# Two PSUM tiles for the transposed squares of layer 1's token tiles, shared out by reading engine instead of by half

## The chip, the cores and the metric

The kernel runs on one core of a Trainium2 chip. The metric is device time in microseconds (us): the median of three runs, 1484.73 us for the kernel before. One execution was also taken by the hardware profiler; the durations in this document come from it.

## The reference

The reference is a model of two layers over 512 latent tokens and 256 context tokens of width 1024 (768 tokens, six tiles of 128). Layer 0 mixes by a long convolution and by attention, layer 1 by a chunked mLSTM. Each layer normalizes the tokens, scales and shifts them by numbers computed from the condition, projects, mixes, and adds the result back:

```python
for layer in range(DEPTH):
    sh_l, sc_l, ga_l = adaln(c, w_mod[layer], b_mod[layer])
    sh_c, sc_c, ga_c = adaln(c_ctx, w_mod[layer], b_mod[layer])
    h_lat = rms_norm(x_lat, g_pre[layer]) * (1 + sc_l[:, None]) + sh_l[:, None]
    h_ctx = rms_norm(x_ctx, g_pre[layer]) * (1 + sc_c) + sh_c
    ...
    x_lat = x_lat + ga_l[:, None] * rms_norm(y_lat, g_post[layer])
```

The change touches the place where layer 1's `h_lat` and `h_ctx` are made and turned round, so that the model dimension lies on the partitions for the projection `h @ w_in`.

## The kernel before, in words

Everything is computed in 32 bits on TensorE by splitting each operand into a high and a low part and taking three products (`mm3`). The program is written in regions. In a region the calls on an engine are first recorded and then issued in an order written out by hand in a table (`record` and `play`, L988 to L1001; tables `ORDERS`, the one for this place is `ORDERS["out0"]`, L436 to L474). `play` also asks for that order to be kept on each engine, so the five engines' own orders are fixed numbers. Every recorded instruction is issued by one helper, which is why all rows of the profile carry its line, L998. The names of tiles tell the rows apart.

Region "out0" is the last part of layer 0: the output projection and, token tile by token tile (4, 5, 0, 1, 2, 3), the function `epi0` (L2203 to L2220). It adds the gated, normalized result to the tokens (`xt`), squares and sums them on ScalarE (`junk`, `ss`), and has VectorE write the normalized tokens in two halves of 512 columns (`xn`). Then comes `h_tile` (L1165 to L1180). For each half, TensorE transposes four squares of 128 x 128 into PSUM (`pm`, written by a matmul with the identity `c_ident`). ScalarE scales and shifts squares 0 and 1 of the half into `hf`, VectorE squares 2 and 3. `hf` holds all eight squares of a token tile and has one buffer. At last `split` (L1003 to L1005) makes the high part `hTh` on ScalarE (a CAST) and the low part `hTl` on VectorE, half by half; both are operands of layer 1's projections.

Between the transposes the order table puts TensorE's other work: the matmuls of layer 0's output projection (`pj` from `yoh`, `yol`), and, once tiles 4, 5, 0 and 1 are split, layer 1's first value projections (`pj` from `hTh`, `hTl`, with 288 columns). VectorE also collects the output projection (`yacc`), splits weights (`wl`), and after the last token tile makes sums (`zs`, `uu`) and the gate inputs (`wa`), which TensorE transposes next.

In the hand order TensorE doesn't transpose a tile's halves one after the other in all cases: in tiles 4, 0 and 3 squares of the two halves come in turns. "The second half" here is the one that comes later in the order.

Waits are set from the tiles: an instruction waits for earlier instructions of other engines on the same PSUM tile, whichever part of it they touch, two reads included. A PSUM tile here is one bank of 512 32-bit numbers on each partition, that is four squares. `pm` has four such places, and a table (`"pm@11"`, L826) says which tile goes to which.

Of the kernel before, what the change touches and what calls it, by code (L numbers as in the profile page):

```python
# [9 lines left out]
AF = mybir.ActivationFunctionType  # L10
ALU = mybir.AluOpType
# [3 lines left out]
P = 128  # L15
# [886 lines left out]
def _body(tc, ins, outs):  # L902
# [9 lines left out]
    def uid(s):  # L912
        cnt[0] += 1
        return f"{s}_{cnt[0]}"
# [13 lines left out]
    def T(pl, tag, shape, dt=F32, bufs=None):  # L928

        b = bufs or bufs_of.get(id(pl)) or 1  # L930
        name = uid(tag)
        if b > 1:
            key = f"{tag}@{pools.setdefault(id(pl), (len(pools), pl))[0]}"
            n = turn_of[key] = turn_of.get(key, -1) + 1
            order = SLOTS.get(key)
            tag, b = f"{tag}_{order[n] if order else n % b}", 1
        kw = {} if bufs is None and b == 1 else {"bufs": b}
        return pl.tile(list(shape), dt, tag=tag, name=name, **kw)

    def PJ(shape=(P, 512)):  # L940
        return T(pp.pj, "pj", shape)

    def PM(shape=(P, 512)):
        return T(pp.pm, "pm", shape) if pp.pm is not pp.pj else PJ(shape)
# [35 lines left out]
    V, S, TE = Engine("vector", pinv), Engine("scalar", pinv), Engine("tensor", pin)  # L980
# [22 lines left out]
    def split(hi, lo, src):  # L1003
        S.copy(hi, src)
        return V.tensor_tensor(lo, src, f(hi), ALU.subtract).ins  # L1005
# [50 lines left out]
    def const(name, shape, dt=F32, src=None, eng=None):  # L1056
        t = cp.tile(list(shape), dt, tag="c_" + name, name="c_" + name)
        (eng or G).dma_start(t, src if src is not None else ins[name])
        return t
# [3 lines left out]
    ident = const("ident", (P, P), eng=S)  # L1063
# [85 lines left out]
    scl = [cp.tile([P, KT, 2], F32, tag=f"scl{l}", name=f"scl{l}") for l in range(2)]  # L1149
    shf = [cp.tile([P, KT, 2], F32, tag=f"shf{l}", name=f"shf{l}") for l in range(2)]  # L1150
# [12 lines left out]
    turns = [[] for _ in range(6)]  # L1163

    def h_tile(pl, i, xn, scl, shf):  # L1165

        c = 0 if i < 4 else 1
        hf = T(pl, "hf", (P, KT, P))
        for hh in range(2):
            ps = PM((P, 4, P))  # L1170
            for t in range(4):
                turns[i].append(TE.transpose(ps[:, t, :], xn[hh][:, t * P:(t + 1) * P], ident).ins)
            for t in range(4):
                ft = hh * 4 + t
                if t < 2:
                    S.activation(hf[:, ft, :], ps[:, t, :], AF.Identity, bias=shf[:, ft, c:c + 1], scale=scl[:, ft, c:c + 1])
                else:
                    V.tensor_scalar(hf[:, ft, :], ps[:, t, :], scl[:, ft, c:c + 1], shf[:, ft, c:c + 1], ALU.mult, ALU.add)
            sl = slice(hh * 4, hh * 4 + 4)
            split(hTh[:, sl, i * P:(i + 1) * P], hTl[:, sl, i * P:(i + 1) * P], hf[:, sl, :])  # L1180

# [5 lines left out]
    def proj_seg(w, c, s):  # L1187

        ps = PJ()
        _, a, n = SEGS[s]  # L1190
        for kt in range(KT):
            mm3(ps[:, :n], tuple(x[:, kt, c * P:(c + 1) * P] for x in w), hcols(kt, a, a + n), kt == 0, kt == KT - 1)
        return ps

    def proj_feat(w, c, turned=False):
        if turned:
            return [proj_seg(w, c, s) for s in (1, 0)][::-1]
        return proj_seg(w, c, 0), proj_seg(w, c, 1)
# [58 lines left out]
    for d in 'x0 x1 z x3 x2 x4 W00 x5 s0 h0 s1 s2 h1 h2 W01 s3 h3 W10 W11'.split():  # L1257
# [13 lines left out]
        elif d[0] == "h":  # L1271
            u = int(d[1])
            if u < 3:
                t = [T(xp, "xt", (P, 4, 256), bufs=6) for _ in range(2)]
            else:
                t = rawa[:, 8:12], rawb[:, 0:4]
# [370 lines left out]
    for j in range(8):  # L1647
        w = load_w(ew[2 * j]) if j else None
        x1c = T(hp, "tmp", (P, NT))
        ps = proj_feat(w, 0) if j else ps0[:2]  # L1650
# [7 lines left out]
        ps = ps0[2:]  # L1658
        if j:
            ps = []  # L1660
# [10 lines left out]
        ps = proj_feat(w, 0)  # L1671
# [14 lines left out]
        for s, a, n in SEGS:  # L1686
            R = n // P
            ps = proj_seg(w, 1, s)
# [27 lines left out]
    for i in range(6):  # L1716
        ps = PJ()[:, :256]
# [54 lines left out]
    for c in range(2):  # L1772
        t = cg[c]
        V.tensor_tensor(t, rope[:, 0], grow[:, c:c + 1].broadcast_to([P, 4, P]), ALU.mult)
        t = sg[c]
# [265 lines left out]
    for n in range(24):  # L2041
# [3 lines left out]
        for b in range(2):  # L2045
# [6 lines left out]
            if n in (18, 19):  # L2052
                c = 2 * (n - 18) + b
# [149 lines left out]
    def epi0(i, rs):  # L2203
        xt = T(op, "xt", (P, D), bufs=2)
        SP.dma_start(xt, ins["x"][i])
        for hf, y in enumerate((yacc0, yacc1)):
            sl = slice(hf * 512, (hf + 1) * 512)
            V.scalar_tensor_tensor(xt[:, sl], y[:, i], rs, xt[:, sl], ALU.mult, ALU.add)
        if i < 4:
            SP.dma_start(x1d[i], xt)  # L2210
        ss = T(op, "ss", (P, 1), bufs=2)
        xn = [T(op, "xn", (P, 512), bufs=3) for _ in range(2)]
        junk = T(op, "junk4", (P, D), mybir.dt.bfloat16, bufs=1)
        S.activation(junk, xt, AF.Square, accum_out=ss)
        rs = T(op, "rs", (P, 1), bufs=2)
        tmp = T(op, "sst", (P, 1), bufs=2)
        rstd(rs, ss, D, tmp)
        for hf in range(2):
            V.tensor_scalar(xn[hf], xt[:, hf * 512:(hf + 1) * 512], rs, None, ALU.mult)
        return lambda: h_tile(op, i, xn, scl[1], shf[1])  # L2220
# [673 lines left out]
```

## Time and profile before

| | us |
|---|---|
| three runs, median (lowest to highest) | 1484.73 (1484.15 to 1485.28) |
| profiled execution, whole | 1486.4 |
| span of its instructions | 1484.6 |
| TensorE (PE) busy in the span | 1448.9 |
| VectorE (DVE) busy | 1071.1 |
| ScalarE (ACT) busy | 778.8 |

The profile was taken at a mean granted TensorE clock of 0.999 of full speed. Busy time is not the same as time on the path to the end: an engine that is busy half the time can still make another wait. The rows further down show which. In a row of the timeline several like instructions in direct sequence stand together (x4); the start is that of the first, the length that of all of them. Matmul ends are modelled and overlap, so matmuls are followed from start to start.

### The profile page before, as it was taken

The numbers are of one execution on the slowest core, as the hardware profiler recorded it, in microseconds if no ns is written. First come the engines' busy times: TensorE is split into PE (matmuls) and PEld (weight loads), VectorE is DVE, ScalarE is ACT, GpSimd is POOL, SyncE is SP. The second block draws the span as 40 slices with busy tenths as digits, with TensorE's granted clock in tenths as the row PEclk, the third lists the DMA queues.
The fourth block names the chain that finished last, engine by engine and source line by source line (L and its number), as shares of the span: only waits on it lengthen the run. The fifth ranks groups of instructions, "written<-read, shape, count | busy, mean of one in ns | idle before, by whom it ended". The sixth has DMA issues, their size and how long they took to land. (4 is left out here: it accounts for less than half of the span.)

```text
span 1484.6 us, 25597 instructions
## 1 busy us (share of the span) xinstructions
PE 1448.9 (98%) x10122; PEld 1320.5 (89%) x10122; DVE 1071.1 (72%) x1971; ACT 778.8 (52%) x1587; POOL 95.2 (6%) x141
## 2 busy tenths in 40 slices
PE   7999999999999999999999989999999999999997
PEld 5888998989998998989997779999999999989776
DVE  6687777887865666668334899666777777778698
ACT  5643443344435444446332567655766666766554
POOL 1100000001000000000000100000000101110000
PEclk9999999999999999999999999999999999999999
DMA  9655556557331121233463343676654647476575
GB/s 380 212 139 151 142 138 165 147 127 185 86 103 43 55 96 47 90 118 104 152 217 98 114 144 129 228 257 211 221 166 114 161 126 166 141 199 179 203 256 215
DMA packets 63687, 230.93 MB, mean 156 GB/s; under 512 B 7707, under 2 KB 9243, under 8 KB 60784
## 3 DMA queue, kind: packets, MB, share of 16 engines
q1 hardware_dynamic: 55000, 198.63, 38.9%
q0 software_dynamic: 7696, 29.50, 11.3%
q8 instruction: 79, 1.29, 0.3%
q10 hardware_dynamic: 872, 1.18, 0.2%
q14 instruction: 40, 0.33, 0.1%
HBM read 207.23 MB, written 68.19 MB: 186 GB/s over the span
## 5 line engine op out<-in xcount | busy, mean ns | idle before, releaser
L998 PE MATMUL pj<-wl,hTh 128*128 128x256 f32 (+2 forms) x1104 | 315.4, 291 | 1.9 <-DVE wl L998 1.9
L998 PE MATMUL pj<-wh,hTh 128*128 128x256 f32 (+2 forms) x1104 | 316.2, 293 | 0.8 <-ACT qjunk L998 0.4
L998 PE MATMUL pj<-wh,hTl 128*128 128x256 f32 (+2 forms) x1104 | 313.8, 291 | 0.0
L998 PE MATMUL pj<-hTh,wh 128*128 128x512 f32 (+1 forms) x832 | 286.7, 347 | 0.1
L998 PE MATMUL pj<-hTl,wh 128*128 128x512 f32 (+1 forms) x832 | 285.5, 344 | 0.6 <-DVE hTl L998 0.6
L998 PE MATMUL pj<-hTh,wl 128*128 128x512 f32 (+1 forms) x832 | 285.2, 345 | 0.0
L998 DVE TENSOR_TENSOR wl<-wr,wh 128x1024 fp32r<-128x1024 f32 (+1 forms) x154 | 187.6, 1222 | 48.5 <-ACT wh L998 45.7
L998 PEld LDWEIGHTS pj<-wl,hTh 128*128 128x128 f32 x1104 | 206.9, 189 | 7.4 <-DVE wl L998 2.9
L998 PEld LDWEIGHTS pj<-wh,hTh 128*128 128x128 f32 x1104 | 205.9, 188 | 7.4 <-issue 2.0
L998 PEld LDWEIGHTS pj<-wh,hTl 128*128 128x128 f32 x1104 | 206.0, 188 | 4.3 <-issue 1.1
L998 ACT CAST wh<-wr 128x1024 fp32r<-128x1024 f32 (+1 forms) x154 | 159.0, 1044 | 95.5 <-PE pj L998 61.7
L998 PEld LDWEIGHTS pj<-hTh,wh 128*128 128x128 f32 x832 | 156.6, 189 | 19.2 <-DVE vl L998 0.9
L998 PEld LDWEIGHTS pj<-hTh,wl 128*128 128x128 f32 x832 | 156.3, 188 | 18.2 <-DVE wl L998 0.2
L998 PEld LDWEIGHTS pj<-hTl,wh 128*128 128x128 f32 x832 | 156.7, 189 | 17.4 <-DVE hTl L998 0.9
L998 DVE TENSOR_TENSOR PTl<-pj,PTh 128x384 fp32r<-128x384 f32 (+1 forms) x80 | 41.1, 525 | 18.8 <-ACT PTh L998 18.3
L998 ACT CAST PTh<-pj 128x384 fp32r<-128x384 f32 (+1 forms) x80 | 35.5, 458 | 30.6 <-PE pj L998 30.0
L998 DVE TENSOR_TENSOR wl<-ch,wh 128x1024 fp32r<-128x1024 f32 x28 | 34.2, 1221 | 24.1 <-ACT wh L998 24.0
L998 DVE TENSOR_REDUCE mx<-s 128x1 f32<-128x768 f32 (+1 forms) x48 | 37.2, 774 | 11.4 <-PE s L998 11.2
L998 PE MATMUL pm<-Rh,dfa 128*128 128x256 f32 (+1 forms) x192 | 44.9, 305 | 0.0
L998 POOL DMA_DIRECT2D o_sums<-in_o_w_in x28 | 22.8, 814 | 333.9 <-DMA o_sums<-in_o_w_in 167.2
L998 DVE TENSOR_TENSOR med<-big 128x512 f32<-128x512 f32 (+1 forms) x48 | 40.4, 865 | 5.0 <-ACT big L998 4.7
L998 PE MATMUL s<-dfa,qTh 128*128 128x256 f32 (+1 forms) x160 | 42.8, 338 | 0.7 <-ACT hdh L998 0.6
(397 smaller groups left out, 3250.3 us busy)
## 6 DMA issues: line engine op xcount, KB each, us to landing
wr<-in_e_w_in SPq DMA_DIRECT2D x52, 512.0 KB, 5.0
wr<-in_o_w_in SPq DMA_DIRECT2D x50, 512.0 KB, 6.4
o_sums<-in_o_w_in POOLq DMA_DIRECT2D x28, 512.0 KB, 6.7
ch<-o_sums SPq DMA_DIRECT2D x21, 512.0 KB, 4.8
wh<-in_w_mod SPq DMA_DIRECT2D x10, 1024.0 KB, 8.4
wl<-in_w_mod SPq DMA_DIRECT2D x9, 1024.0 KB, 7.6
wr<-in_e_w_out SPq DMA_DIRECT2D x16, 512.0 KB, 4.0
w_sums<-in_o_w_out POOLq DMA_DIRECT2D x16, 512.0 KB, 7.6
```

Source lines behind the costliest of these rows:

```text
L998: x = fn(*a, **k)
```

## The change

Before, each half of a token tile has a PSUM tile of its own, and ScalarE and VectorE both read from it. After, the two PSUM tiles are taken at the head of the function; one receives squares 0 and 1 of both halves, which ScalarE reads, the other squares 2 and 3 of both halves, which VectorE reads. The arithmetic, the number of instructions and each engine's order stay the same.

```diff
--- before.py
+++ after.py
@@ -1166,16 +1166,17 @@
 
         c = 0 if i < 4 else 1
         hf = T(pl, "hf", (P, KT, P))
+        pair = [PM((P, 4, P)) for _ in range(2)]
         for hh in range(2):
-            ps = PM((P, 4, P))
             for t in range(4):
-                turns[i].append(TE.transpose(ps[:, t, :], xn[hh][:, t * P:(t + 1) * P], ident).ins)
+                turns[i].append(TE.transpose(pair[t // 2][:, 2 * hh + t % 2, :], xn[hh][:, t * P:(t + 1) * P], ident).ins)
             for t in range(4):
                 ft = hh * 4 + t
+                ps = pair[t // 2][:, 2 * hh + t % 2, :]
                 if t < 2:
-                    S.activation(hf[:, ft, :], ps[:, t, :], AF.Identity, bias=shf[:, ft, c:c + 1], scale=scl[:, ft, c:c + 1])
+                    S.activation(hf[:, ft, :], ps, AF.Identity, bias=shf[:, ft, c:c + 1], scale=scl[:, ft, c:c + 1])
                 else:
-                    V.tensor_scalar(hf[:, ft, :], ps[:, t, :], scl[:, ft, c:c + 1], shf[:, ft, c:c + 1], ALU.mult, ALU.add)
+                    V.tensor_scalar(hf[:, ft, :], ps, scl[:, ft, c:c + 1], shf[:, ft, c:c + 1], ALU.mult, ALU.add)
             sl = slice(hh * 4, hh * 4 + 4)
             split(hTh[:, sl, i * P:(i + 1) * P], hTl[:, sl, i * P:(i + 1) * P], hf[:, sl, :])
 
```

What differs in the program is which tile an instruction names, and so which waits it carries. The marks DVE_49, Activation_49 and PE_49 are the semaphores of VectorE, ScalarE and TensorE. First TensorE at token tile 4, as a difference (`pm_8126` and `pm_8127` are the tile's two PSUM tiles, `xn_8108` and `xn_8109` its halves, `pj` lines are output projection):

```order
-L998 MATMUL pm_8126<-c_ident,xn_8108 128x128 [waits DVE_49]
-L998 MATMUL pm_8126<-c_ident,xn_8108 128x128 x3
+L998 MATMUL pm_8126<-c_ident,xn_8108 128x128 [waits DVE_49,Activation_49]
+L998 MATMUL pm_8126<-c_ident,xn_8108 128x128
+L998 MATMUL pm_8127<-c_ident,xn_8108 128x128 x2
 L998 MATMUL pj_8124<-wh_1254_8096,yoh_8027 128x512
-L998 MATMUL pm_8127<-c_ident,xn_8109 128x128 [waits Activation_49]
-L998 MATMUL pm_8127<-c_ident,xn_8109 128x128 x2
+L998 MATMUL pm_8126<-c_ident,xn_8109 128x128 [waits Activation_49]
+L998 MATMUL pm_8127<-c_ident,xn_8109 128x128 [waits DVE_49]
+L998 MATMUL pm_8127<-c_ident,xn_8109 128x128
```

The transposes stand at the same places of TensorE's order; two of them now name the other PSUM tile, and three carry a wait for a reader where one did.

Next TensorE at token tile 2 (`pm_8185`, `pm_8186`; second half `xn_8165`), again as a difference, between value projections:

```order
 L998 MATMUL pj_8196<-wl_1349_8191,hTh 128x288
 L998 MATMUL pj_8196<-wh_1348_8190,hTl 128x288
+L998 MATMUL pm_8185<-c_ident,xn_8165 128x128 [waits Activation_49]
+L998 MATMUL pm_8185<-c_ident,xn_8165 128x128
 L998 MATMUL pm_8186<-c_ident,xn_8165 128x128 [waits DVE_49]
-L998 MATMUL pm_8186<-c_ident,xn_8165 128x128 x3
+L998 MATMUL pm_8186<-c_ident,xn_8165 128x128
 L998 MATMUL pj_8196<-wh_1348_8190,hTh 128x288
```

Of the four transposes of the second half two go to the first half's tile of before, and the first of them has a wait for ScalarE.

Last ScalarE at token tiles 2 and 3 (`hf_8184`, `hf_8187`), before:

```order
L998 ACTIVATE hf_8184<-pm_8185,shf_71,scl_69 128x128 [waits DVE_49,PE_49,Activation_49]
L998 ACTIVATE hf_8184<-pm_8186,shf_71,scl_69 128x128 [waits PE_49]
L998 ACTIVATE hf_8184<-pm_8185,shf_71,scl_69 128x128
L998 ACTIVATE hf_8184<-pm_8186,shf_71,scl_69 128x128 [waits DVE_49]
L998 CAST hTh<-hf_8184 128x4x128 [waits Activation_49]
L998 CAST hTh<-hf_8184 128x4x128 [waits DVE_49]
L998 ACTIVATE hf_8187<-pm_8189,shf_71,scl_69 128x128 [waits DVE_49,PE_49]
L998 ACTIVATE hf_8187<-pm_8188,shf_71,scl_69 128x128 [waits DVE_49]
```

and after:

```order
L998 ACTIVATE hf_8184<-pm_8185,shf_71,scl_69 128x128 [waits DVE_49,PE_49,Activation_49]
L998 ACTIVATE hf_8184<-pm_8185,shf_71,scl_69 128x128 [waits PE_49]
L998 ACTIVATE hf_8184<-pm_8185,shf_71,scl_69 128x128 x2
L998 CAST hTh<-hf_8184 128x4x128 [waits DVE_49,Activation_49] x2
L998 ACTIVATE hf_8187<-pm_8188,shf_71,scl_69 128x128 [waits DVE_49,PE_49]
L998 ACTIVATE hf_8187<-pm_8188,shf_71,scl_69 128x128 x3
L998 CAST hTh<-hf_8187 128x4x128 [waits DVE_49,Activation_49]
L998 CAST hTh<-hf_8187 128x4x128 [waits DVE_49]
```

ScalarE's reads of a token tile follow one another without a wait for VectorE between them, and the splits (CAST) now carry the wait for VectorE's reads that earlier reads had carried.

## Rows read from the trace of the kernel before

**Rows 1.** The page's first part: busy time of each engine, its share of the span, and its instructions.
```profile
PE 1448.9 (98%) x10122; PEld 1320.5 (89%) x10122; DVE 1071.1 (72%) x1971; ACT 778.8 (52%) x1587; POOL 95.2 (6%) x141
```

**Rows 2.** The table by windows, for the stretch around the token tiles and for all that follows: window and its length, then busy us (and instructions) of PE, PEld, DVE, ACT and POOL, the granted clock, the DMA share and GB/s.
```profile
825.00:880.00 55.00, 48.56 (x272) 40.77 (x271) 47.48 (x103) 33.66 (x69) 8.91 (x15) 1.00 0.41 143
...
880.00:1484.00 604.00, 589.86 (x4215) 546.16 (x4213) 459.04 (x806) 379.70 (x783) 39.89 (x65) 1.00 0.60 184
```

**Rows 3.** The table of waits of 825 to 880 us: who waited, for whom, us in total, times, the longest.
```profile
PE pm L998 <- DVE xn L998: 4.0, 5, 1.0
ACT hf L998 <- DVE hf L998: 3.8, 3, 2.1
...
DVE hf L998 <- ACT hf L998: 2.4, 4, 1.0
...
PE pm L998 <- DVE wa L998: 1.6, 1, 1.6
```

**Rows 4.** The view of the tile `hf`: engine, operation and count, then least, median and longest ns of one, first and last start, and shape.
```profile
L998 ACT ACTIVATE hf<-pm,shf,scl x24: 441/456/459, 834.0 to 872.2; 128x128 f32<-128x128 f32 x24
...
L998 ACT CAST hTh<-hf x12: 605/620/622, 836.8 to 873.2; 128x512 fp32r<-128x512 f32 x12
```

**Rows 5.** The timeline around tile 4. Here and in the groups up to 10 the columns are start and length in us, engine, line, operation, out<-in, shapes and count; in brackets the idle time before it and what ended that.
```profile
834.89 0.49 PE L998 MATMUL pm<-c_ident,xn 128*128 128x128 f32 x3
834.96 1.06 ACT L998 ACTIVATE junk<-xt 128x1024 bf16<-128x1024 f32 x1 [0.55 <-DVE xt L998]
836.01 0.79 ACT L998 ACTIVATE hf<-pm,shf,scl 128x128 f32<-128x128 f32 x2
836.21 0.72 DVE L998 TENSOR_SCALAR hf<-pm,scl,shf 128x128 f32<-128x128 f32 x2
836.62 0.39 PE L998 MATMUL pj<-wl,yoh 128*128 128x512 f32 x1
836.86 0.40 PE L998 MATMUL pj<-wh,yol 128*128 128x512 f32 x1
837.50 0.33 PE L998 MATMUL pm<-c_ident,xn 128*128 128x128 f32 x1 [0.25 <-DVE xn L998]
```

**Rows 6.** The timeline at tile 5's reads and up to the first transposes of tile 0.
```profile
841.83 0.41 DVE L998 TENSOR_SCALAR hf<-pm,scl,shf 128x128 f32<-128x128 f32 x1 [0.30 <-ACT hf L998]
842.27 0.81 ACT L998 ACTIVATE hf<-pm,shf,scl 128x128 f32<-128x128 f32 x2 [0.48 <-DVE hf L998]
844.16 1.05 ACT L998 ACTIVATE junk<-xt 128x1024 bf16<-128x1024 f32 x1
847.16 0.81 PE L998 MATMUL pm<-c_ident,xn 128*128 128x128 f32 x4 [0.87 <-DVE xn L998]
```

**Rows 7.** The timeline at tile 0.
```profile
847.61 1.20 ACT L998 ACTIVATE hf<-pm,shf,scl 128x128 f32<-128x128 f32 x3 [1.55 <-PE pm L998]
848.86 0.55 PE L998 MATMUL pm<-c_ident,xn 128*128 128x128 f32 x3 [0.55 <-ACT hf L998]
852.26 0.68 DVE L998 TENSOR_TENSOR yacc<-pj,yacc 128x512 f32<-128x512 f32 x1
```

**Rows 8.** The timeline at tile 1, up to the first transpose of tile 2.
```profile
858.57 0.46 ACT L998 ACTIVATE hf<-pm,shf,scl 128x128 f32<-128x128 f32 x1 [0.64 <-PE pm L998]
859.38 0.48 DVE L998 TENSOR_SCALAR xn<-xt,rs 128x512 f32<-128x512 f32 x1
859.92 0.33 PE L998 MATMUL pm<-c_ident,xn 128*128 128x128 f32 x1 [1.00 <-DVE xn L998]
```

**Rows 9.** The timeline at tile 2, and the first transposes of tile 3 (866.85 and 869.16).
```profile
862.41 0.60 PE L998 MATMUL pm<-c_ident,xn 128*128 128x128 f32 x4
864.26 0.40 PE L998 MATMUL pj<-wl,hTh 128*128 128x288 f32 x1 [0.31 <-DVE wl L998]
864.79 0.68 DVE L998 TENSOR_TENSOR hTl<-hf,hTh 128x512 fp32r<-128x512 f32 x1
865.57 0.29 PE L998 MATMUL pj<-wl,hTh 128*128 128x288 f32 x1
865.70 0.29 PE L998 MATMUL pj<-wh,hTl 128*128 128x288 f32 x1
866.43 1.74 ACT L998 ACTIVATE hf<-pm,shf,scl 128x128 f32<-128x128 f32 x4 [2.12 <-DVE hf L998]
866.85 0.30 PE L998 MATMUL pm<-c_ident,xn 128*128 128x128 f32 x1 [0.85 <-DVE xn L998]
867.27 0.41 DVE L998 TENSOR_SCALAR hf<-pm,scl,shf 128x128 f32<-128x128 f32 x1 [0.56 <-ACT hf L998]
869.16 0.52 PE L998 MATMUL pm<-c_ident,xn 128*128 128x128 f32 x3 [0.98 <-DVE xn L998]
```

**Rows 10.** The timeline at tile 3's reads and splits, and at the gates' first transpose.
```profile
871.71 1.08 DVE L998 TENSOR_SCALAR hf<-pm,scl,shf 128x128 f32<-128x128 f32 x3 [0.98 <-ACT hf L998]
873.29 1.29 DVE L998 TENSOR_TENSOR hTl<-hf,hTh 128x512 fp32r<-128x512 f32 x2 [0.50 <-ACT hTh L998]
878.80 0.30 PE L998 MATMUL pm<-c_ident,wa 128*128 128x128 f32 x1 [1.62 <-DVE wa L998]
```

**Rows 11.** The table by windows at the end of the span (columns as in Rows 2).
```profile
1476.00:1478.00 2.00, 0.31 (x2) 0.00 (x0) 1.73 (x6) 1.44 (x4) 0.56 (x1) 1.00 0.00 0
...
1481.00:1482.00 1.00, 0.00 (x0) 0.00 (x0) 0.48 (x1) 0.00 (x0) 0.00 (x0) 0.74 1.03 387
```

## The prediction

> **What bounds the kernel now.** I read the busy shares first [rows 1]: TensorE is busy 98% of the span, so another engine counts only where TensorE stands still for it. The table by windows comes next [rows 2]. In 825 to 880 us, where the six token tiles of layer 1 are made, TensorE is busy 48.56 of 55.00 us, so 6.44 us idle; in the 604 us behind it, 589.86. The reader is to see that this stretch has idle time to lose and to swallow, and that what is late at its end finds little room later. The table of waits of the stretch [rows 3] names the idle time: TensorE's transposes wait 4.0 us in five places for VectorE's normalized halves `xn`, 1.6 us once for `wa`, and only once for a read of the squares, 0.55 us [rows 7]. The waits between the two readers are larger, 3.8 us of ScalarE for VectorE and 2.4 us of VectorE for ScalarE. Last come the timelines of the tiles, in the order 4, 5, 0, 1, 2, 3 [rows 5 to 10].
>
> **What is removed, and what is added.** No instruction comes or goes and no engine's order changes; the wait marks move. Before, the two readers of one PSUM tile took turns, whichever engine stood first in the program. After, each reads its own tile, so the 3.8 and 2.4 us can go. But now the second half's two squares for ScalarE go into the tile from which ScalarE reads the first half's, and VectorE's likewise. TensorE's transposes of the second half therefore wait for reads of the first half, where before they had a tile of their own. Behind a waiting transpose stand all projection matmuls, since TensorE has one queue. A read lasts 0.456 us on ScalarE [rows 4] and 0.41 on VectorE [rows 6], two in a row 0.79 and 0.72 [rows 5], and the follower on another engine starts about 0.05 us after the end (the `xn` that ends at 859.86 and the transpose at 859.92 [rows 8]). I take +0.05 as the hand-over.
>
> *Tile 4* [rows 5]. The second half's transposes start at 834.89. ScalarE's two reads of the first half run from 836.01 to 836.80, behind its square-sum of 1.06 us at 834.96. New start: 836.80 + 0.05 = 836.85, +1.96. TensorE idled 0.25 at 837.50; the matmul before started at 836.86 and the next could follow 0.23 us later (836.62, 836.86), at 837.09, so 0.41 to 0.50 comes back, I take 0.45: +1.5. VectorE's reads of that half, from 836.21, wait for the late squares: 837.38, its queue about +1.06.
>
> *Tiles 5 and 0, entry* [rows 6]. TensorE's +1.5 meets its 0.87 wait at 847.16 for `xn`. VectorE, 1.06 us late, waited 0.30 us at 841.83 for a read of ScalarE, and ScalarE 0.48 us at 842.27 for VectorE; both waits go. ScalarE, whose square-sum at 844.16 sets VectorE's next steps, then catches up some 0.6 us. VectorE's `xn` is 0.47 late. TensorE follows at +0.38, as its transpose there waits for one engine where it waited for two, to which I give 0.09.
>
> *Tile 0* [rows 7]. The first pair of squares for ScalarE goes out at 847.16 + 0.38 = 847.54. In the rows ScalarE's read starts 0.45 us after that (847.61), so here at 847.99, and two reads together last some 0.81 [rows 6]: to 848.80. The other half's pair for ScalarE went out third in the group of four, near 847.56; it now waits for those reads, 848.80 + 0.05, and 0.09 for a second wait mark (the same choice of mine as at the entry), 848.94: +1.38. The old wait of 0.55 at 848.86 goes, so +0.69 there. The last pair for VectorE, near 849.0 before, waits for VectorE's two reads of the tile, 849.93 to 850.66: 850.71, some +1.7. VectorE's `yacc` of 852.26 waits for those projections: +1.65, so both engines are now late alike.
>
> *Tile 1* [rows 8]. TensorE waits some 0.7 us more for ScalarE's read at 858.57, and its 1.00 us wait at 859.92 swallows it: still +1.65.
>
> *Tile 2* [rows 9]. This is the largest wait. The second half goes out at 862.41, early, into an empty tile. After, it needs ScalarE's first read of the tile, and that read waits for tile 1's last `hTl` on VectorE (864.79 + 0.68 = 865.47), because `hf` has one buffer. So 865.47 + 1.65 + 0.12 = 867.24, the read ends at 867.70, and the transposes start at 867.74: +5.33, where it would have come to them at 862.41 + 1.65 = 864.06; less the tail of the matmul before, 0.3 us, TensorE stands idle for 3.4 us. Then it has 2.9 us of projections. There matmuls start every 0.13 us (865.57, 865.70), so the places with 0.31 and 0.85 us idle are worth 0.45 and 0.98 from start to start, and the one with 0.98 us at 869.16 is worth 1.13: +3.90 at 866.85, +2.77 at 869.16. On VectorE the hand-over of 0.56 goes; its third read moves from 867.27 to 868.43 (+1.16), and the last `xn` is only 0.55 late.
>
> *Tile 3* [rows 10]. The first half's squares come 2.77 late, the fourth, some 0.5 behind the group's start at 869.16, at 872.4. Before, the readers took turns (0.98 at 871.71, 0.50 at 873.29); after, they don't. VectorE's first read starts at 872.79, 0.1 behind the square's end; it lasts 0.41, and the last transpose, in VectorE's tile, follows at 873.32. That square is ready at 873.60, VectorE's three reads go from 873.63 to 874.6, ScalarE's cast of the first half (0.62 [rows 4]), behind VectorE's second read, from 874.13 to 874.75, and `hTl` starts at 874.71, where it was 873.29: +1.42. All of VectorE up to `wa` follows in a row, and TensorE's wait of 1.62 us at 878.80 swallows the difference between 2.77 and 1.42. Behind 880 TensorE is nearly full, so +1.42 stays.
>
> **The sum.** 1.96 - 0.45 (tile 4), - 1.12 (entry of tile 0), + 1.26 (tile 0), 0 (tile 1), + 3.69 (tile 2 at its worst), - 2.56 (its idle places), - 1.35 (tile 3 and `wa`): +1.4 us. The profiled execution took 1486.4 us around a span of 1484.6, and would take 1487.8; it lies 1.67 above the runs' median of 1484.73, so in the runs I expect 1484.73 + 1.42 = **1486.2 us**. No row shows TensorE waiting for a whole half's reads in this way. From below, all removed turns pay and no new wait binds: -(2.4 + 0.55) = -2.95. From above, tile 2's wait arrives whole: +5.3. I take +1.4, nearest the rows, since the two waits that decide (834.89 and 862.41) have every start and length in a row.
>
> The turn-taking that goes is there in rows: at 871.71 VectorE stands still 0.98 us until ScalarE has read its square of the same tile [rows 10]. The Trainium skill (PSUM — Partial Sum Buffer, "PSUM bank collisions raise a hardware error") says that any two engines on one bank must be kept apart, reads by ScalarE and VectorE too; the trace agrees. Against the change speaks another sentence of the Trainium skill (Perfetto Trace Analysis, "Optimizing Tensor Performance / Matmuls"): independent matmul groups should rotate through PSUM banks so that the evacuation of one lies beside the next group. By the first alone the sum would be -2.95, by the second alone up to +5.3.
>
> **Rivals.**
> *The removed turns pay (faster).* TensorE's own wait of 0.55 and VectorE's 2.4 us are gone, and `xn`, the most frequent releaser, comes from VectorE: in full 1481.8, at half 1483.3. Against it: at 834.96 ScalarE is in a square-sum, so its reads can't come earlier, and 862.41 lies before the buffer `hf` is free.
> *The stall of tile 2 isn't swallowed (slower).* The idle places at 866.85 and 869.16 take in 2.6 us only if VectorE's `xn` stays under 0.6 us late. VectorE reads a square at 868.43 before that `xn`; if TensorE's transposes come 1 us later than I have, every us goes on to `xn`, tile 3 and `wa`. It decides from a third VectorE read after 869.4: then +2.8 to +5.3, 1487.5 to 1490.0, middle 1488.6. For it: three engines wait on each other in a ring there. Against it: at 866.43 ScalarE starts sooner without VectorE's turn.
> *The clock.* TensorE would stand still 3.4 us once. At the end of the program the granted clock is still 1.00 (2.4 GHz) in 1476 to 1478, with 0.31 us of matmuls, and 0.74 on average only in 1481 to 1482 [rows 11], so a longer pause than 3.4 us shows no fall at first. If it did fall to 1.2 GHz, the 2.9 us of matmuls behind the pause would take twice as long: 1489.1. The Trainium skill (TensorE: Matmul & The Clock Gate, "Part 1: The HAM clock gate") tells that an idle TensorE is set back to 1.2 GHz; by that rule this rival would come true, and the rows at the end say only that it isn't at once.
> *No change.* The change may not do what it says to the time: waits of TensorE and of the readers cancel, 1484.7. For it: `wa` at 878.80 is set by VectorE, which loses about as many waits as it gains.
>
> **How the numbers follow.** Chances: the forecast 0.56 (own range 1485.2 to 1487.4), removed turns pay 0.11 (half of it beyond 0.2%), the stall 0.14 (four fifths beyond), the clock 0.07, no change 0.12. A measurement here can tell 0.2%, which is 2.97 us, from no change: faster is below 1481.8, slower above 1487.7. So faster 0.05; slower 0.11 + 0.07 + 0.03 of the forecast's upper tail = 0.21; same 0.74. The range 1483.3 to 1488.9 leaves out the full gain below and the upper part of the stall and clock cases above, some 0.2.
>
> **What would show it.** Right: ScalarE and VectorE wait for each other's reads of `hf` under 1 us in all; TensorE's transposes wait for ScalarE and VectorE reads in tiles 4, 0 and 2, the longest wait about 3.4 us near 864 to 868; the wait for `wa` near 880 falls to about 0.3 us; the lateness is +1.5 at tile 5, +0.4 at tile 0, +1.65 at tile 1 and +1.4 behind `wa`; the windows behind 880 keep TensorE's busy time. Wrong: no wait of TensorE over 1 us at tile 2, or the last `hTl` of tile 3 more than 2.5 us late or not late at all, or a granted clock under 1.00 near 870.

## The result and the profile after

The changed kernel took 1488.91 us (median of nine runs, 1487.98 to 1490.2), the kernel before on the same occasion 1485.21 us. The ratio is 1.0026 with a 95% interval of 1.0016 to 1.0036, so +3.9 us (+2.4 to +5.3). A second comparison gave 1.0023 (1.0014 to 1.0032), +3.4 us. The forecast of +1.4 us, within 0.2%, was too small; the median lies just above the upper end of the range, 1488.9.

First the page and the table by windows of the kernel after, as [rows 1, 2]; the second window starts 3 us later, so that it holds the same work.

```profile
PE 1450.6 (98%) x10122; PEld 1322.2 (89%) x10122; DVE 1070.8 (72%) x1971; ACT 779.7 (52%) x1587; POOL 95.7 (6%) x141
```

```profile
825.00:883.00 58.00, 50.05 (x274) 42.31 (x273) 47.71 (x103) 33.67 (x69) 8.74 (x15) 0.97 0.39 136
883.00:1487.00 604.00, 590.09 (x4214) 546.45 (x4212) 458.73 (x806) 380.23 (x783) 40.48 (x65) 1.00 0.59 184
```

Behind 883 nothing is different (590.09 us of TensorE for 589.86). In front of it TensorE is idle 7.95 us where it was 6.44, and the granted clock of the stretch is 0.97 where it was 1.00: two things, not one. TensorE's busy time in the stretch is 1.5 us longer, with 274 matmuls for 272.

The table of waits of 825 to 884 us, as [rows 3]:

```profile
PE pm L998 <- ACT hf L998: 6.5, 4, 3.5
...
DVE hf L998 <- PE pm L998: 5.5, 6, 2.3
...
ACT hf L998 <- DVE hTl L998: 1.3, 1, 1.3
...
PE pm L998 <- DVE hf L998: 0.8, 1, 0.8
...
PE pm L998 <- DVE wa L998: 0.3, 1, 0.3
```

The readers no longer wait for each other (3.8 and 2.4 us before). In their place TensorE's transposes wait 6.5 us for ScalarE's reads and 0.8 us for VectorE's. The timeline of TensorE (first and last row: the first transpose of the token tiles, and the gate inputs' transpose, which serve as marks below):

```profile
833.84 0.27 PE L998 MATMUL pm<-c_ident,xn 128*128 128x128 f32 x1
...
837.07 0.55 PE L998 MATMUL pm<-c_ident,xn 128*128 128x128 f32 x3 [1.53 <-ACT hf L998]
...
849.17 0.44 PE L998 MATMUL pm<-c_ident,xn 128*128 128x128 f32 x2 [0.90 <-ACT hf L998]
...
850.88 0.44 PE L998 MATMUL pm<-c_ident,xn 128*128 128x128 f32 x2 [0.82 <-DVE hf L998]
...
861.82 0.33 PE L998 MATMUL pm<-c_ident,xn 128*128 128x128 f32 x1 [0.22 <-DVE xn L998]
...
868.00 1.12 PE L998 MATMUL pm<-c_ident,xn 128*128 128x128 f32 x4 [3.52 <-ACT hf L998]
...
881.62 0.30 PE L998 MATMUL pm<-c_ident,wa 128*128 128x128 f32 x1 [0.33 <-DVE wa L998]
```

The stand-still of 3.52 us at token tile 2 is there, where and as long as forecast. What released it stands in the rows of VectorE and ScalarE, which are cut from two timelines:

```profile
866.68 0.68 DVE L998 TENSOR_TENSOR hTl<-hf,hTh 128x512 fp32r<-128x512 f32 x1
```

```profile
867.48 0.46 ACT L998 ACTIVATE hf<-pm,shf,scl 128x128 f32<-128x128 f32 x1 [1.28 <-DVE hTl L998]
```

`hTl` of token tile 1 ends at 867.36, ScalarE's read starts 0.12 later, and TensorE goes on 0.06 after the read's end at 867.94. Behind that the windows show the granted clock:

```profile
866.00:867.00 1.00, 0.00 (x0) 0.00 (x0) 1.00 (x4) 0.20 (x2) 0.09 (x1) 1.00 1.05 373
867.00:868.00 1.00, 0.01 (x1) 0.01 (x1) 0.89 (x3) 0.46 (x1) 0.77 (x1) 0.69 1.10 205
868.00:869.00 1.00, 1.00 (x5) 1.00 (x6) 0.60 (x2) 0.28 (x1) 0.00 (x0) 0.50 0.76 156
...
870.00:871.00 1.00, 1.00 (x7) 1.00 (x6) 0.85 (x2) 0.91 (x2) 0.24 (x3) 0.60 0.99 401
871.00:872.00 1.00, 1.00 (x9) 1.00 (x9) 0.71 (x2) 0.00 (x0) 0.00 (x0) 1.00 1.02 406
```

TensorE has stood still since 864.48. The clock falls to 0.50, which is 1.2 GHz, within the window from 867 to 868, before TensorE has any work again, and TensorE then works at that pace until nearly 871. The matmuls of 288 columns show it from start to start:

```profile
869.39 0.44 PE L998 MATMUL pj<-wh,hTl 128*128 128x288 f32 x1
869.63 0.44 PE L998 MATMUL pj<-wh,hTh 128*128 128x288 f32 x1
...
870.96 0.29 PE L998 MATMUL pj<-wh,hTh 128*128 128x288 f32 x1
871.09 0.29 PE L998 MATMUL pj<-wl,hTh 128*128 128x288 f32 x1
```

0.24 us at 0.50, 0.13 us at 1.00. The Trainium skill (TensorE: Matmul & The Clock Gate, "Part 1: The HAM clock gate") says that an idle TensorE is set back to 1.2 GHz; here the trace agrees, with 0.50 behind 3.52 us without work.

### The profile page after: what moved, and what is told of

The parts are those of the page before. It is cut to its first block, busy times and chain, and to the rows that moved or that the text cites. A ratio compares the mean times of both kernels' runs of the same rounds, so it can differ in the third digit from the quotient of the medians.

```text
span 1487.7 us, 25593 instructions
## 1 busy us (share of the span) xinstructions
PE 1450.6 (98%) x10122; PEld 1322.2 (89%) x10122; DVE 1070.8 (72%) x1971; ACT 779.7 (52%) x1587; POOL 95.7 (6%) x141
```

## The experiments

Outside the stretch between the two marks below, single profiles differ by up to 5.3 us (the span less the distance: 1436.0 us with 7 fill matmuls, 1441.2 with hf in two halves). So each is measured by its own marks: from the first transpose of the token tiles to the gate inputs' transpose. Before, that is 878.80 - 833.64 = 45.16 us. All the kernels, by start of both marks and their distance:

```
kernel                       first     gates    distance  against before  longest stand-still, lowest clock
before                       833.64    878.80    45.16        -           1.62   1.00
after                        833.84    881.62    47.78      +2.62         3.52   0.50
after, second profile        832.04    881.29    49.25      +4.09         3.52   0.50
after, third                 831.94    881.10    49.16      +4.00         3.52   0.50
after, fourth                833.01    882.05    49.04      +3.88         3.52   0.50
tile 2 by halves             833.21    879.25    46.04      +0.88         1.51   1.00
only tile 2 by reader        831.73    879.37    47.64      +2.48         3.52   0.50
14 fill matmuls              833.25    879.78    46.53      +1.37         1.67   1.00
7 fill matmuls               831.67    878.21    46.54      +1.38         2.60   1.00
transposes moved back        833.40    878.80    45.40      +0.24         1.52   1.00
hf in two halves             832.87    881.54    48.67      +3.51         2.82   0.50
hf in two halves, second     832.98    881.68    48.70      +3.54         2.83   0.50
four PSUM tiles              832.50    873.90    41.40      -3.76         0.97   1.00
four, and hf in two halves   833.00    874.01    41.01      -4.15         0.95   1.00
```

The theory was that the loss is the new wait of token tile 2 (+1.4 with the smaller waits) and the clock behind it (+1.2). The rivals: tiles 4 and 0 make the loss, or the clock is only a mark beside a wait that I had sized too small.

### Which token tile

Token tile 2 by halves again, the others as changed; the second kernel is the other way round, with 'pair' for token tile 2 and 'half' for the others. The lines are cut from the difference to the changed kernel:

```diff
+        how = {4: 'pair', 5: 'pair', 0: 'pair', 1: 'pair', 2: 'half', 3: 'pair'}[i]
...
-                turns[i].append(TE.transpose(pair[t // 2][:, 2 * hh + t % 2, :], xn[hh][:, t * P:(t + 1) * P], ident).ins)
+                if how == "pair":
+                    at[t] = pair[t // 2][:, 2 * hh + t % 2, :]
+                elif how == "half":
+                    at[t] = pair[hh][:, t, :]
...
+                turns[i].append(TE.transpose(at[t], xn[hh][:, t * P:(t + 1) * P], ident).ins)
```

> The tiles are shared out by reader in five token tiles; token tile 2 alone has its squares by halves, as in the kernel before. Theory (the new wait of tile 2 and the fall of the clock behind it make up most of the loss): TensorE waits nowhere more than 1.6 us near the token tiles, the granted clock is 1.00 throughout 825 to 883 us, and the kernel is +0.8 us against the kernel before. Rival (the waits of tiles 4 and 0 make the loss): it stays at +2.6 us or more, with the clock at 1.00.

> Only token tile 2 is shared out by reader, the other five are by halves. Theory: one stand-still of TensorE of some 3.4 us near 863 to 866, the granted clock at 0.50 for some 3 us behind it, and +1.1 from the wait plus +1.2 from the clock, +2.3 us in all against the kernel before. Rival (tiles 4 and 0): under +0.5 us.

Without tile 2 the distance is +0.88 (expected +0.8), at a clock of 1.00, and the time is the same as before (ratio 0.9998, 0.9989 to 1.0007). Tile 2 alone gives +2.48 (expected +2.3), and in time 1.0014 (1.0003 to 1.0024). Its stand-still and the windows around its end:

```profile
864.15 0.85 PE L998 MATMUL pm<-c_ident,xn 128*128 128x128 f32 x4 [3.52 <-ACT hf L998]
```

```profile
864.00:865.00 1.00, 0.84 (x5) 0.78 (x6) 0.76 (x3) 0.47 (x3) 0.00 (x0) 0.79 0.89 168
865.00:866.00 1.00, 1.00 (x6) 1.00 (x5) 0.96 (x3) 1.00 (x4) 0.00 (x0) 0.50 0.77 242
866.00:867.00 1.00, 1.00 (x6) 1.00 (x6) 0.84 (x3) 0.81 (x2) 0.24 (x3) 0.50 0.98 401
```

The rival of tiles 4 and 0 falls: the wait of 1.5 us at tile 4 and the two of 0.9 and 0.8 at tile 0 are all in the first of these kernels, and are swallowed or paid with 0.9 us.

### What the clock costs by itself

Fill matmuls whose products nobody reads go to TensorE right ahead of the waiting transposes of tile 2, 14 of them and in a second kernel 7. The line makes them, and the table of the order puts them there (its rows are written on one line in these kernels, so that the helper stands at L960 in their profiles):

```diff
+    for k in range(14):
+        TE.matmul(pairs[3][0].rearrange("p c t -> p (c t)")[:, :288], hTh[:, 0, 5 * P:6 * P], wv0[0][:, 0, :], start=True, stop=True)
```

> The changed kernel with 14 more matmuls of 288 columns (products that nobody reads, written to a PSUM tile that the next token tile overwrites) ahead of the waiting transposes of token tile 2; they take some 1.9 us of a stand-still of 3.5 us. Theory (the clock costs 1.2 us by itself): the granted clock stays at 1.00, the transposes start where they did, and the kernel is +1.4 us against before, though it does more work than the changed kernel. Rival (the wait alone makes the loss, the clock is a mark beside it): the time of the changed kernel, +2.6 us or more.

> The changed kernel with 7 fill matmuls of 288 columns in place of the 14 of the earlier run: TensorE stands still some 2.6 us in place of 3.5 (and 1.67 with 14). Waits alone: +1.4 us. If a stand-still of that length brings the clock down as 2.82 us did with hf in halves: +2.6 to +4.1 in the profile, clock at 0.50 for 3 us or more. If it doesn't: +1.4 and 1.00. I expect a fall, since 2.6 is nearer to 2.82 than to 1.67.

With 14 the transposes start 867.38 - 833.25 = 34.13 us behind the first mark, in the changed kernel 868.00 - 833.84 = 34.16: the wait ends at the same place. But the clock stays up:

```profile
867.38 0.70 PE L960 MATMUL pm<-c_ident,xn 128*128 128x128 f32 x4 [1.67 <-ACT hf L960]
```

```profile
866.00:867.00 1.00, 0.00 (x0) 0.00 (x0) 0.89 (x4) 0.13 (x1) 0.70 (x1) 1.00 1.04 258
867.00:868.00 1.00, 0.62 (x5) 0.56 (x6) 0.98 (x3) 0.47 (x2) 0.16 (x1) 1.00 1.00 209
868.00:869.00 1.00, 1.00 (x10) 1.00 (x10) 0.88 (x3) 1.00 (x4) 0.00 (x0) 1.00 0.83 229
```

The distance is +1.37, my own sum for the waits, and a kernel with more work is faster than one with less: in time 1.0002 (0.9992 to 1.0013) against 1.0026. That separates the two parts; the rival that the wait alone makes the loss falls. With 7 I was wrong: I expected a fall after a stand-still of 2.6 us, and there was none; +1.38 and 1.0003 (0.9994 to 1.0012):

```profile
865.83 0.70 PE L960 MATMUL pm<-c_ident,xn 128*128 128x128 f32 x4 [2.60 <-ACT hf L960]
```

```profile
865.00:866.00 1.00, 0.17 (x2) 0.18 (x2) 0.89 (x4) 0.46 (x1) 0.61 (x1) 1.00 1.02 188
866.00:867.00 1.00, 1.00 (x9) 0.93 (x9) 0.86 (x4) 0.70 (x2) 0.00 (x0) 1.00 1.02 176
```

### Work that stands behind the wait

The four transposes of tile 2's second half go behind the 18 projection matmuls that followed them, by the table of the order (893 to 896 are the transposes; the other engines' instructions keep their own order):

```diff
-..., 961, 893, 894, 895, 896, 962, 963, 964, 965, 966, 967, 898, 900, 968, ...
+..., 961, 962, 963, 964, 965, 966, 967, 968, ..., 946, 893, 894, 895, 896, 898, 900, ...
```

> The changed kernel with the four waiting transposes of token tile 2 moved behind the 18 projection matmuls that stood behind them on TensorE; nothing else moves. Theory (the loss is work that stands behind a wait): TensorE waits under 1.5 us there, the granted clock stays at 1.00, and the kernel is within +0.5 us of before (worked out: +0.1). Rival (the chain of VectorE and ScalarE is what is late, whatever TensorE has queued): +1.4 us or more.

+0.24 (expected +0.1), clock 1.00, the same time as before (1.0002, 0.9991 to 1.0012). Around tile 2 TensorE now waits 0.76 us for `wl` and 0.53 us for a read of VectorE, and stands still nowhere else there:

```profile
865.71 0.40 PE L960 MATMUL pj<-wl,hTh 128*128 128x288 f32 x1 [0.76 <-DVE wl L960]
...
871.59 0.33 PE L960 MATMUL pm<-c_ident,xn 128*128 128x128 f32 x1 [0.53 <-DVE hf L960]
```

So ScalarE's read was not late by itself; what cost time was TensorE's work queued behind a transpose that had to wait for it.

### The one buffer of hf

`hf` as two tiles, one for each half, in the same memory:

```diff
-        hf = T(pl, "hf", (P, KT, P))
+        hfp = [T(pl, f"hf{q}", (P, 4, P)) for q in range(2)]
```

> The changed kernel, but hf is two tiles of half the size (one for each half of a token tile, the same memory), so that ScalarE's first read of token tile 2 waits for the first of tile 1's two hTl subtractions on VectorE and not for the second, 0.66 us later. Theory (the stand-still is set by the one buffer of hf, and the clock falls only after the long stand-still): the stand-still is 2.8 to 2.9 us, the granted clock stays at 1.00, and the transpose of the gate inputs comes +1.2 us late against the kernel before, +1.2 us in the time. If the stand-still is shorter and the clock falls all the same: +2.4. Rival (the buffer isn't what ScalarE waits for): 3.5 us as in the changed kernel, and +2.6.

> The changed kernel with hf in two tiles of half the size, a second profile (the first had a stand-still of 2.82 us and the clock at 0.50 for some 6.5 us). Theory (the fall comes with a stand-still of this length in some or all executions and costs 1.2 or 2.5 us): the gate inputs' transpose +1.2 us late without a fall, +2.4 or +3.7 with one.

The stand-still is 2.82 us in place of 3.52, 0.70 shorter (expected 0.66): it is the buffer of `hf` that ScalarE's read waits for. What I had not expected is that the clock falls all the same, and for longer:

```profile
866.33 1.44 PE L998 MATMUL pm<-c_ident,xn 128*128 128x128 f32 x4 [2.82 <-ACT hf L998]
```

```profile
865.00:866.00 1.00, 0.00 (x0) 0.00 (x0) 1.00 (x4) 0.41 (x3) 0.07 (x1) 0.72 1.06 389
866.00:867.00 1.00, 0.67 (x2) 0.29 (x2) 1.00 (x4) 0.27 (x1) 0.79 (x1) 0.50 1.14 209
...
871.00:872.00 1.00, 1.00 (x7) 0.98 (x6) 0.00 (x0) 0.00 (x0) 0.00 (x0) 0.50 0.99 401
872.00:873.00 1.00, 1.00 (x9) 1.00 (x8) 0.00 (x0) 0.00 (x0) 0.00 (x0) 0.87 1.03 422
```

+3.51 and +3.54 in the two profiles, 1.0020 (1.0010 to 1.0030) in time. If the waits alone make +1.2 us here, as worked out, the slow clock makes the other 2.3; the shorter stand-still bought nothing that the times show.

### The same kernel again

> The changed kernel as it is, beside the others on the same chip. Theory (waits +1.4, clock +1.2): the gate inputs' transpose +2.6 us late against the kernel before, the granted clock at 0.50 for about 3 us, the time +2.6. Rival (the fall of the clock was a matter of one execution): a second profile with the clock at 1.00 and +1.4.

> The changed kernel once more, a third profile: after two profiles with the granted clock at 0.50 for some 3 us and some 6.5 us behind the stand-still of token tile 2. Theory (the stand-still always brings the clock down, and only how long it stays down differs from one execution to the next): a stand-still of 3.5 us, then the clock at 0.50 for 3 or for 6 to 7 us, the gate inputs' transpose +2.6 or +4.1 us late. Rival (the clock falls in some executions only): at least one further profile with the clock at 1.00 and +1.4.

> The changed kernel a fourth time, for the same question: theory, the clock at 0.50 for 3 or for 6 to 7 us and +2.6 or +4.1 us; rival, 1.00 throughout and +1.4 us.

In all four profiles of the changed kernel the stand-still is 3.52 us and the clock falls. The rival, a profile at 1.00 and +1.4, did not turn up. In three of the four the clock stays at 0.50 for longer than in the first. The second one's windows:

```profile
865.00:866.00 1.00, 0.00 (x0) 0.00 (x0) 0.89 (x2) 0.32 (x1) 0.86 (x1) 0.73 1.18 225
866.00:867.00 1.00, 0.80 (x5) 0.81 (x5) 0.80 (x3) 0.22 (x2) 0.00 (x0) 0.50 0.88 176
...
871.00:872.00 1.00, 1.00 (x6) 0.98 (x6) 0.00 (x0) 0.00 (x0) 0.00 (x0) 0.50 1.03 422
872.00:873.00 1.00, 1.00 (x9) 0.98 (x8) 0.00 (x0) 0.00 (x0) 0.00 (x0) 0.86 0.90 369
```

Against the +1.38 of the fill kernels the clock costs 1.24 us in the first and 2.71, 2.62 and 2.50 us in the others. The mean of the four distances is +3.65 us, and the two timed comparisons gave +3.9 and +3.4. My figure of +2.6 for the changed kernel came from the first profile alone; that part of the theory was too small.

The timed runs, each of which has a mean granted clock over its whole span, point the same way: 0.9966 on average over the twenty timed runs of the changed kernel, 0.9983 over the runs of the kernel before in the second comparison. The difference of 0.0017 over 1487 us makes some 5 us at half clock, an estimate that lies between the short and the long falls of the profiles. (Falls elsewhere are in these means too: the fourth profile has 0.83 in 1330 to 1340.) With fill matmuls the runs have 0.9980 (14 of them) and 0.9982 (7), the kernel before 0.9984 on both occasions.

### Both gains without the price

Four PSUM tiles for each token tile, one for each half and reader, each half filled (there are four places for `pm`, so each token tile takes all of them); then also `hf` in two tiles. `more` are two further PSUM tiles at places named by hand; the lines are cut from the difference to the changed kernel:

```diff
+        how = {4: 'four', 5: 'four', 0: 'four', 1: 'four', 2: 'four', 3: 'four'}[i]
...
+        more = [pp.pm.tile([P, 4, P], F32, tag=f"pm_{q}", name=uid("pm")) for q in {4: [0, 1], 5: [2, 3], 0: [0, 1], 1: [2, 3], 2: [0, 1], 3: [2, 3]}[i]] if how == "four" else None
...
+                    at[t] = (pair, more)[t // 2][hh][:, t, :]
```

> Each token tile has four PSUM tiles, one for each half and each reader, each half filled; neither the readers' turns nor the waits of the second half for the first half's reads are there. Theory (the change gained by the turns and lost by the new waits and the clock): no wait of TensorE for reads of hf over 0.5 us, no waits of ScalarE and VectorE for each other's reads over 0.5 us in all, clock 1.00, the gate inputs' transpose 3.6 us earlier than before, so -3 to -3.6 us in the time. Rival (the turns were hidden anyway): within 1 us of before.

> As the run with four PSUM tiles for each token tile, and hf in two tiles of half the size. Theory: another 0.4 us earlier, -4.0 us at the gate inputs' transpose. Rival (the buffer of hf is off the path once the PSUM waits are gone): the same as with four tiles alone.

The distance is -3.76 us (expected -3.6), and in time 0.9975 (0.9966 to 0.9985): 1481.91 us against 1485.59, faster than both kernels. The two marks, and the table of waits of the stretch:

```profile
832.50 0.27 PE L998 MATMUL pm<-c_ident,xn 128*128 128x128 f32 x1
...
873.90 0.33 PE L998 MATMUL pm<-c_ident,wa 128*128 128x128 f32 x1 [0.69 <-DVE wa L998]
```

```profile
ACT hf L998 <- DVE hTl L998: 2.2, 2, 1.3
PE pm L998 <- DVE xn L998: 1.7, 3, 1.0
...
PE pm L998 <- DVE wa L998: 0.7, 1, 0.7
PE pm L998 <- ACT hf L998: 0.7, 1, 0.7
```

The readers' waits for each other are gone from it, and the granted clock is 1.00 throughout the stretch. TensorE still waits 0.67 us for ScalarE once, where token tile 2 takes over a place from which ScalarE reads token tile 1; I had put the limit at 0.5. ScalarE's wait for `hTl` is still there too, but no transpose waits behind it. With `hf` in halves as well it is -4.15 (expected -4.0, one profile each), and in time 0.9976 (0.9966 to 0.9985), which can't be told from the other: whether the buffer of `hf` still counts there stays open. This is the sentence of the Trainium skill that spoke against the change (Perfetto Trace Analysis, "Optimizing Tensor Performance / Matmuls"), applied: groups that don't depend on each other in banks of their own. The trace agrees, with the -3.76 us.

## Why the prediction was wrong

The steps up to tile 2 held. Lateness against the first mark, forecast and measured (after, less the 0.20 us by which its first mark is later):

- Tile 4: the second half's transposes at 837.07, against 834.89 before: +1.98, forecast +1.96.
- Tile 1 to 2: 861.82 against 859.92: +1.70, forecast +1.65. The first transpose of tile 0 came +0.50 late, forecast +0.38. Behind it the second pair of transposes for ScalarE starts at 848.97 (849.17 less the 0.20), forecast 848.94, and this is luck in part: the 0.09 that I gave a second wait mark is in no row (ScalarE's reads end at 848.31 + 0.81 = 849.12, 0.05 before the transposes), and it stood in my sum twice, with opposite signs.
- Tile 2: 868.00 against 862.41: +5.39, forecast +5.33, with the stand-still of 3.52 for 3.4. That ScalarE's read is held by the one buffer of `hf` is shown by the run with `hf` in halves.
- The swallowing behind it: with the clock held up by fill matmuls the gate inputs' transpose is +1.37 and +1.38 late, forecast +1.42. So the idle places took in what I had said they would. With 14 fill matmuls the steps hold one by one (starts of this kernel, plus the 0.39 us by which its first mark is earlier): tile 3's transposes come +3.86 and +2.67 late, forecast +3.90 and +2.77, and tile 3's last `hTl` pair +1.37, forecast +1.42.

```profile
870.32 0.27 PE L960 MATMUL pm<-c_ident,xn 128*128 128x128 f32 x1
...
871.44 0.49 PE L960 MATMUL pm<-c_ident,xn 128*128 128x128 f32 x3
...
874.27 1.30 DVE L960 TENSOR_TENSOR hTl<-hf,hTh 128x512 fp32r<-128x512 f32 x2
```

- Behind 880 nothing changes in the windows, as forecast.

The step that failed is the clock behind the stand-still. My sum has no term for it: I gave it 0.07 as a rival, and it came true in all four profiles, with 1.24 to 2.71 us behind a wait that I had sized rightly. Two of my signs of being wrong came with it: tile 3's last `hTl` pair is 2.62 us late, where I had drawn the line at 2.5, and the granted clock is under 1.00 near 870. My reason was the end of the program, where the granted clock is still 1.00 in 1476 to 1478 and falls only in 1481 to 1482 [rows 11]. I read one late fall as a rule that a pause of 3.4 us would pass. In the changed kernel the clock was at 0.69 on average in the 1 us row of the table that begins 2.5 us after TensorE's last matmul, with `hf` in halves at 0.72 in one that begins 1.5 us after it, and with only tile 2 by reader at 0.79 in one that begins 3.4 us after it. One fall at the end of one trace is a single sample of when a pause shows, and it can't bound another pause. I had priced the rival at +2.9 us, 1489.1 us in all; the four profiles show 1.24 to 2.71 us, and the time was 1488.91. The size was about right for three of them and more than twice too large for the first; the chance was not right. (The middle of my stall rival, 1487.5 to 1490.0, is 1488.75 and not 1488.6, which changes nothing.)

The rival that the stall isn't swallowed did not happen: VectorE's third read at tile 2 starts at 869.15, before my mark of 869.4 and, less the 0.20, 1.68 us late for 1.16 forecast. The excess is the clock's: in the kernel with 14 fill matmuls, where the clock stays at 1.00, the same read is 1.24 us late (868.12). At -2.95 for the removed turns alone I was also too small: with four tiles they are worth 3.76 us. I had left ScalarE's 3.8 us out of that sum as off the path; they hold back `hTh` and with it VectorE, which may be the difference, but no run takes that apart.

What stays open: why the slow clock lasts about 3 us behind the stand-still in one profile and some 6 us in three, and why 2.60 us (fill) brought no fall where 2.82 us did. The eleven timed runs with 7 fill matmuls (mean clock 0.9982, time 1.0003 of before) show that the missing fall is not a matter of one profile. It is no limit even so: other work stood ahead of the two pauses, and no run varies the length alone.

## What to carry to other kernels

In a program like this one, whose waits go by the whole PSUM tile, a tile that two engines read makes them take turns (3.8 and 2.4 us here); a tile that is written in two steps and read by one engine makes TensorE wait for that engine (6.5 and 0.8 us). Splitting by reader alone trades the first for the second, and the second stands in the one queue on the path; look for places enough to split by both. Where a change makes TensorE stand still for about 3 us, put a price on the clock behind it, from rows at either clock (0.24 and 0.13 us for the same matmul here), and don't rule it out by one late fall elsewhere.

## What the runs showed that I had not expected

The same stand-still of 3.52 us cost 1.24 us of slow clock in one execution and 2.50 to 2.71 in three others. And work that nobody reads made the kernel faster: 14 matmuls of 288 columns, 1.9 us of TensorE, took the time from 1.0026 to 1.0002 of before, because TensorE went on at 2.4 GHz.
